# Plain float32 products for the first values, and reciprocal roots by logarithm and exponential on ScalarE

## The chip, the cores and the metric

The kernel runs on one core of a Trainium2 chip. The engines of the core are TensorE (PE in the profile; PEld is its weight load), VectorE (DVE), ScalarE (ACT), GpSimd (POOL) and SyncE (SP), which issues most of the transfers. The metric is the device time of one execution in microseconds; lower is better. The kernel before takes 343.04 us, the median of three runs (342.67 to 343.07).

## What is computed

A decoder trunk on 256 tokens of width 1024, all in float32: a mixer of four attention kinds with four heads each, a cross-attention into 256 memory tokens, and a squared-ReLU MLP of width 4096. Cut to what matters here:

```python
def rmsnorm(x, g):
    y = x * lax.rsqrt(jnp.mean(x * x, axis=-1, keepdims=True) + NORM_EPS)
    return y * g

x = x + hybrid_mixer(rmsnorm(x, g_mix), w_in, g_group, sinks, w_out, rel_table)
x = x + memory_cross_attention(rmsnorm(x, g_cross), rmsnorm(mem, g_mem), w_xq, w_xkv, w_xo)
x = x + jnp.square(jax.nn.relu(rmsnorm(x, g_mlp) @ w_up)) @ w_down
return rmsnorm(x, g_final)
```

In the mixer, h @ w_in gives queries, keys and values of the groups a (dilated windows), b (stick-breaking), c (sliding window with sinks) and d (one causal block). Each group's result is normed as well, y * rsqrt(mean(y * y) + NORM_EPS), before the output projection.

## The kernel before

The 256 tokens are two row tiles of 128, x0 and x1. The width of 1024 is eight blocks of 128, over which a product sums. A product in full precision is made of three float32r products: each operand is split into a high part (`hi`, a rounding copy on ScalarE, line 314 for weights, 400 for activations) and a residue (`lo`, a subtraction on VectorE, lines 315 and 401), and hi*hi, hi*lo and lo*hi are added in PSUM (lines 424 to 426). Weights come in halves of 512 KB into one of four `raw` buffers (line 300), and each half is split into two of the fifteen `w` buffers.

Start: x0, the first half of the weights of group a's values (`av`), x1, the second half, and the query weights `aq` are loaded in that order by SyncE, the first gain by ScalarE's queue. Forty small products on a tile of zeros (line 366, called warm-ups below) run on TensorE meanwhile, wherever nothing else can. Each row tile is transposed by TensorE (line 407), multiplied by the gain on VectorE (line 417) into `tmp`, and split. The norm's root does not stand before the products: it scales queries and keys as a row (`rq`, `rk`, lines 462 and 463; `spread` on line 459 turns it by a transpose) and values as a column (line 498). The values of group a are 48 products for both tiles (line 495), with a piece of the relative bias between them (line 471).

A reciprocal root (`rstd_of`, lines 383 to 388): ScalarE squares a row with a running sum (line 392), VectorE makes the variance (line 385), GpSimd raises it to the power -0.5 (line 386). There are sixteen of these: two at the start, two for the memory rows, eight for the attention results (four groups, two tiles), two before the cross-attention, two before the MLP, where GpSimd also squares the root (line 819). The final norm does the same on lines 1001 and 1003, and scales the rows on lines 1014 and 1017.

The order of each engine's instructions comes from a planner (`Plan`): every operation is recorded with an estimated cost and what it reads and writes, and a list scheduler puts them in order by these costs, by ranks and by when buffers come free. So an operation with another engine or cost moves others too. Each engine runs its list strictly in that order. From about 165 us on the MLP runs: sixteen units of 256 hidden columns, fourteen of them by a scheme of seven products in place of eight (`load_s`, `up_s`, `down_s`), the first and the last by the plain scheme.

## Time and profile before

| | |
|---|---|
| median of the runs | 343.04 us |
| the profiled execution | 342.83 us |
| its span | 340.9 us |
| TensorE busy with products | 329.0 us (97%) |
| VectorE busy | 299.2 us (88%) |
| ScalarE busy | 231.7 us (68%) |
| GpSimd busy | 27.6 us (8%) |
| transfers | 59.88 MB, mean 176 GB/s |

The span goes from the first instruction to the last; the rest of the execution's time lies around it. The busy time of an engine is the time in which it had an instruction running. Products are pipelined, so that the duration on record of one is longer than the distance to the next; in a dense stream the distance is what a product costs. A view by stretches tells what is full where, and the list of waits what an engine stood idle for.

### The profile page before, as it was taken

Reading aid. Unit: us, or ns where it says so; the run is one execution under the profiler, and the core shown is the slowest. Engines: PE = TensorE matmul, PEld = TensorE weight load, DVE = VectorE, ACT = ScalarE, POOL = GpSimd, SP = SyncE. Lnnn points to the kernel's source line nnn. Section 1 sums busy time; section 2 is a strip of 40 time slices with the busy share of each in tenths; the row PEclk is TensorE's granted clock in tenths of the full one; section 3 lists DMA queues with packets and bytes.
Section 4 is the critical chain, followed back from the end, with each engine's and each line's share of the span. In section 5 each row is a group of like instructions: output and inputs, shape, how many; then the busy total and the mean of one; then the engine's idle time right before and its main releaser. Section 6 shows DMA issues by size and latency. Waiting matters only on the chain.

```text
span 340.9 us, 6081 instructions
## 1 busy us (share of the span) xinstructions
PE 329.0 (97%) x2326; PEld 302.4 (89%) x2326; DVE 299.2 (88%) x488; ACT 231.7 (68%) x371; POOL 27.6 (8%) x46
## 2 busy tenths in 40 slices
PE   7799999999999999999999999999999999999992
PEld 6699899999898789998998899888999889998882
DVE  3758779779998499878999999999999999999994
ACT  4578857369794476883885876778668678665822
POOL 6422000000121002200020000000000000000000
PEclk9999999999999999999999999999999999999997
DMA  7989775640137334847743646476566574644003
GB/s 257 317 254 330 218 201 181 236 137 0 64 109 214 112 122 147 268 143 227 268 139 109 222 160 232 147 229 198 178 225 211 178 248 159 212 123 125 3 0 123
DMA packets 39757, 59.88 MB, mean 176 GB/s; under 512 B 1990, under 2 KB 32896, under 8 KB 39728
## 3 DMA queue, kind: packets, MB, share of 16 engines
q1 hardware_dynamic: 38928, 57.49, 52.2%
q0 software_dynamic: 640, 1.80, 1.8%
q8 instruction: 18, 0.29, 0.4%
q10 hardware_dynamic: 160, 0.20, 0.2%
q14 instruction: 11, 0.09, 0.1%
HBM read 58.42 MB, written 1.07 MB: 175 GB/s over the span
## 4 chain that ended last, share of the span: by engine, by line
PE 57%; DVE 21%; ACT 7%; issue 7%; DMA 5%; POOL 1%; SPq 0%; POOLq 0%; ACTq 0%; DVEq 0%
PE ps L425 9%; PE ps L424 9%; PE ps L426 9%; PE acc L424 8%; PE acc L425 8%; PE acc L426 8%; DVE w L315 5%; DVE w L872 4%; DMA raw<-in_w_in_dram 3%; PE ps L557 3%; PE ps L407 3%; DMA x<-in_x_dram 2%; ACT w L314 2%; DVE tmp L878 2%; POOL rstd L386 1%
## 5 line engine op out<-in xcount | busy, mean ns | idle before, releaser
L315 DVE TENSOR_TENSOR w<-raw,w 128x1024 fp32r<-128x1024 f32 x72 | 86.1, 1218 | 11.6 <-ACT w L314 8.2
L314 ACT ACTIVATE w<-raw 128x1024 fp32r<-128x1024 f32 x72 | 73.9, 1053 | 14.8 <-PE acc L425 7.6
L425 PE MATMUL ps<-hTlo,w 128*128 128x256 f32 x256 | 72.1, 281 | 0.0
L424 PE MATMUL ps<-hThi,w 128*128 128x256 f32 x256 | 71.9, 281 | 0.0
L426 PE MATMUL ps<-hThi,w 128*128 128x256 f32 x256 | 71.8, 281 | 0.0
L424 PEld LDWEIGHTS ps<-hThi,w 128*128 128x128 f32 x256 | 48.2, 188 | 0.7
L425 PEld LDWEIGHTS ps<-hTlo,w 128*128 128x128 f32 x256 | 48.1, 188 | 0.6
L426 PEld LDWEIGHTS ps<-hThi,w 128*128 128x128 f32 x256 | 48.3, 189 | 0.0
L424 PE MATMUL acc<-w,yThi 128*128 128x512 f32 (+1 forms) x112 | 45.2, 404 | 0.0
L425 PE MATMUL acc<-w,yThi 128*128 128x512 f32 (+1 forms) x112 | 43.7, 390 | 0.0
L426 PE MATMUL acc<-w,yTlo 128*128 128x512 f32 (+1 forms) x112 | 43.7, 390 | 0.0
L871 ACT ACTIVATE w<-tmp 128x1024 fp32r<-128x1024 f32 x28 | 29.6, 1058 | 15.6 <-DVE tmp L881 13.1
L424 PE MATMUL acc<-hThi,w 128*128 128x256 f32 x128 | 36.6, 286 | 0.0
L425 PE MATMUL acc<-hTlo,w 128*128 128x256 f32 x128 | 36.1, 282 | 0.0
L426 PE MATMUL acc<-hThi,w 128*128 128x256 f32 x128 | 35.8, 280 | 0.0
L872 DVE TENSOR_TENSOR w<-tmp,w 128x1024 fp32r<-128x1024 f32 x28 | 34.1, 1218 | 0.0
L386 POOL TENSOR_TENSOR rstd<-var,mhalf 128x1 f32<-128x1 f32 x16 | 15.9, 998 | 137.5 <-DVE var L385 89.4
L426 PEld LDWEIGHTS acc<-w,yTlo 128*128 128x128 f32 x112 | 21.0, 188 | 5.0
L425 PEld LDWEIGHTS acc<-w,yThi 128*128 128x128 f32 x112 | 21.1, 188 | 4.2
L424 PEld LDWEIGHTS acc<-w,yThi 128*128 128x128 f32 x112 | 21.1, 188 | 4.0
L424 PEld LDWEIGHTS acc<-hThi,w 128*128 128x128 f32 x128 | 24.1, 188 | 0.4
L426 PEld LDWEIGHTS acc<-hThi,w 128*128 128x128 f32 x128 | 24.2, 189 | 0.0
(189 smaller groups left out, 708.6 us busy)
## 6 DMA issues: line engine op xcount, KB each, us to landing
raw<-in_w_up_dram SPq DMA_DIRECT2D x32, 512.0 KB, 4.2
raw<-in_w_in_dram SPq DMA_DIRECT2D x22, 512.0 KB, 4.9
hThi<-in_w_down_dram SPq DMA_DIRECT2D x14, 512.0 KB, 3.4
hTlo<-in_w_down_dram SPq DMA_DIRECT2D x14, 512.0 KB, 4.1
raw<-in_w_out_dram SPq DMA_DIRECT2D x8, 512.0 KB, 3.4
raw<-in_w_xkv_dram SPq DMA_DIRECT2D x4, 512.0 KB, 3.5
raw<-in_w_down_dram SPq DMA_DIRECT2D x4, 512.0 KB, 4.3
w<-dstrip POOLq DMA_DIRECT2D x3, 512.0 KB, 8.3
```

The source lines that it names most:

```text
L314: act(1024, lambda raw=raw, hi=hi: nc.scalar.activation(hi.t, raw.t, AF.Copy), [raw], [hi])
L315: dve(1024, lambda raw=raw, hi=hi, lo=lo: nc.vector.tensor_sub(lo.t, raw.t, hi.t.bitcast(F32)), [raw, hi], [lo])
L386: pool(0.5, lambda: nc.gpsimd.tensor_tensor(r.t, v.t, mhalf.t, op=ALU.pow), [v, mhalf], [r])
L407: nc.tensor.transpose(dst[:, tsl(k)], view()[:, tsl(k)], ident.t)
L424: nc.tensor.matmul(dst, lh, rh, start=start, stop=False)
L425: nc.tensor.matmul(dst, lh, rl, start=False, stop=False)
L426: nc.tensor.matmul(dst, ll, rh, start=False, stop=stop)
L557: nc.tensor.matmul(view()[:, h, :], z[:, i, :], v[:, j, kv(h), :], start=j == 0, stop=j == len(pT[h]) - 1)
L871: act(512 * n, lambda: nc.scalar.activation(hi.t, view(), AF.Copy), [key], [hi])
L872: dve(512 * n, lambda: nc.vector.tensor_sub(lo.t, view(), hi.t.bitcast(F32)), [key, hi], [lo])
L878: dve(1024, lambda: nc.vector.tensor_sub(s.t, raw[:, 1:2].to_broadcast([P, 2, 512]), raw[:, 0:4:3]), [raw], [s])
```

## The change

The first values (group a) are no longer computed from split operands: their weights go as they come into two `w` buffers (`load_whole`), and the products take the gained, transposed rows `tmp` themselves, in plain float32, 16 of them with a planned cost of 0.43 us each. So the weights of `av` are not split; x0 and x1 still are, for queries and keys. The planner's cost of x1's load is raised. The load of the first gain is recorded ahead of x0's; it stays on ScalarE's queue.

A reciprocal root is made by two activations on ScalarE, exp(-0.5 * ln(ssq / n + eps)), with eps as a column in memory (it stands in the buffer named `mhalf`). The MLP's scale, the square of the root, becomes a variance and a reciprocal on VectorE. The factor for the cross-attention's queries (`rs`) moves from GpSimd to VectorE. In the final norm the logarithm takes the sum's last part and, as its bias, the part so far. The first addition to the relative bias no longer waits for the second tile's variance.

```diff
--- before.py
+++ after.py
@@ -32,6 +32,7 @@
 FRONT = 20.0
 EARLY = 1.0
 NUDGE = 0.5
+FULL = 0.43
 LAST = 2
 SPLIT = 640
 LASTC = 768
@@ -326,7 +327,7 @@
         xt.append(buf(f"x{t}", [P, D]))
 
     def load_x(t):
-        dma(P * D * 4, lambda: nc.sync.dma_start(xt[t].t, a["x"][0, tsl(t), :]), [], [xt[t]])
+        dma(P * D * (4 + 3 * t), lambda: nc.sync.dma_start(xt[t].t, a["x"][0, tsl(t), :]), [], [xt[t]])
 
     GN = ("g_mix", "g_cross", "g_mem", "g_mlp")
     grow = [buf("grow0", [KB, P]), buf("grow1", [3 * KB, P])]
@@ -336,14 +337,21 @@
         dma(4096, lambda: eng.dma_start(
             grow[i > 0].t[j:j + KB, :], a[GN[i]][0].rearrange("(k p) -> k p", p=P)), [], [(grow[i > 0], i)])
 
+    whole = []
+
+    def load_whole(part):
+
+        whole.append(buf("w", [P, KB // 2, 256], F32, SPL))
+        dma(P * D * 4, lambda: nc.sync.dma_start(whole[part].t, units["av"][:, 4 * part:4 * part + 4]), [], [whole[part]])
+
+    load_gain(0, nc.scalar)
     load_x(0)
-    load_gain(0, nc.scalar)
-    load("av", 0)
+    load_whole(0)
     load_x(1)
-    load("av", 1)
-    ident, mhalf, warm = buf("ident", [P, P]), buf("mhalf", [P, 1]), buf("warm", [P, 512], BF16)
+    load_whole(1)
+    ident, eps, warm = buf("ident", [P, P]), buf("mhalf", [P, 1]), buf("warm", [P, 512], BF16)
     pool(0.5, lambda: make_identity(nc, ident.t), [], [ident])
-    pool(0.05, lambda: nc.gpsimd.memset(mhalf.t, -0.5), [], [mhalf])
+    pool(0.05, lambda: nc.gpsimd.memset(eps.t, EPS), [], [eps])
     dve(512, lambda: nc.vector.memset(warm.t, 0.0), [], [warm])
     onehot, rel, smask = buf("q", [32, STRIP], F32, 2), buf("rel", [32, NROW]), buf("k", [NROW, STRIP], F32, 2)
     sink, nsink = buf("sink", [P, 4]), buf("nsink", [P, 4])
@@ -378,19 +386,20 @@
     gains_T(0)
 
 
-    last = []
-
     def rstd_of(ssq, n):
-        v, r = buf("var", [P, 1], F32, 4), buf("rstd", [P, 1], F32, 16)
-        dve(1, lambda: nc.vector.tensor_scalar(v.t, ssq.t, 1.0 / n, EPS, op0=ALU.mult, op1=ALU.add), [ssq], [v])
-        pool(0.5, lambda: nc.gpsimd.tensor_tensor(r.t, v.t, mhalf.t, op=ALU.pow), [v, mhalf], [r])
-        last.append(v)
+        r = buf("rstd", [P, 1], F32, 16)
+        v = buf("var", [P, 1], F32, 4)
+        act(1, lambda: nc.scalar.activation(v.t, ssq.t, AF.Ln, bias=eps.t, scale=1.0 / n), [ssq, eps], [v], 1)
+        act(1, lambda: nc.scalar.activation(r.t, v.t, AF.Exp, scale=-0.5), [v], [r], 1)
         return r
 
-    def rstd_row(src, view, n, behind=[]):
+    def ssq_row(src, view, n, behind=[]):
         sq, ssq = buf("sq", [P, D], BF16, 1), buf("ssq", [P, 1], F32, 4)
         act(n, lambda: nc.scalar.activation(sq[:, 0:n], view(), AF.Square, accum_out=ssq.t), [src] + behind, [sq, ssq], 1)
-        return rstd_of(ssq, n)
+        return ssq
+
+    def rstd_row(src, view, n):
+        return rstd_of(ssq_row(src, view, n), n)
 
     def pair(tag, n, bufs):
         return tuple(buf(tag + x, [P, n, S], F32R, bufs) for x in ("hi", "lo"))
@@ -418,6 +427,7 @@
                 tmp[:, ks, :], pt.t.rearrange("p (k t) -> p k t", k=4), gT[g > 0][:, max(g - 1, 0), ks, None].to_broadcast([P, 4, P]),
                 op=ALU.mult), [pt, gT[g > 0]], [(tmp, n)])
             split_to(hl, (t, n), (slice(None), ks, tsl(t)), (tmp, n), lambda ks=ks: tmp[:, ks, :], 512)
+        return tmp
 
     def mm3(dst, l, r, start, stop):
         (lh, ll), (rh, rl) = l, r
@@ -446,9 +456,9 @@
 
 
     h1 = pair("hT", KB, 2)
-    r1 = []
+    g1, r1 = [], []
     for t in range(2):
-        gained_T(xt[t], 0, h1, t)
+        g1.append(gained_T(xt[t], 0, h1, t))
         r1.append(rstd_row(xt[t], lambda t=t: xt[t].t, D))
 
     rq, rk = buf("rq", [P, S]), buf("rk", [P, S])
@@ -469,7 +479,7 @@
     pst0 = pst()
     dstrip = buf("dstrip", [NROW, STRIP], pool=dram)
     pe(0.65, lambda: nc.tensor.matmul(pst0[:NROW, :STRIP], rel.t, onehot.t, start=True, stop=True), [rel, onehot], [pst0])
-    dve(STRIP, lambda: nc.vector.tensor_add(smask.t, pst0[:NROW, :STRIP], smask.t), [pst0, smask, last[-1]], [smask])
+    dve(STRIP, lambda: nc.vector.tensor_add(smask.t, pst0[:NROW, :STRIP], smask.t), [pst0, smask], [smask])
     dma_late(20000, lambda: nc.gpsimd.dma_start(dstrip.t, smask.t), [smask], [dstrip])
 
 
@@ -488,13 +498,10 @@
                 if gi:
                     proj(pv, lambda pv=pv: pv[:, 0:256], n + "v", h1, t)
                 else:
-                    for half in range(2):
-                        for p in ((0, 0), (1, 0), (0, 1)):
-                            for kk in range(4 * half, 4 * half + 4):
-                                w, j = wt("av", kk)
-                                pe(0.109, lambda p=p, kk=kk, w=w, j=j, t=t, pv=pv: nc.tensor.matmul(
-                                    pv[:, 0:256], h1[p[0]][:, kk, tsl(t)], w[p[1]][:, j], start=kk == 0 and p == (0, 0),
-                                    stop=kk == KB - 1 and p == (0, 1)), [w[p[1]], (h1[p[0]], (t, half))], [pv])
+                    for kk in range(KB):
+                        pe(FULL, lambda kk=kk, t=t, pv=pv: nc.tensor.matmul(
+                            pv[:, 0:256], g1[t][:, kk, :], whole[kk // 4][:, kk % 4], start=kk == 0, stop=kk == KB - 1),
+                            [whole[kk // 4], (g1[t], kk // 4)], [pv])
                 act(256, lambda t=t, pv=pv: nc.scalar.activation(
                     v[:, t, :, 0:E], pv[:, 0:256].rearrange("p (h e) -> p h e", h=4), AF.Copy, scale=r1[t].t),
                     [pv, r1[t]], [(v, t)], 1)
@@ -776,7 +783,7 @@
         residual(pacc[t], t)
         gained_T(xt[t], 1, h2, t)
         r2, rs = rstd_row(xt[t], lambda t=t: xt[t].t, D), buf("rs", [P, 1], F32, 2)
-        pool(0.1, lambda r2=r2, rs=rs: nc.gpsimd.tensor_scalar(rs.t, r2.t, -0.125, None, op0=ALU.mult), [r2], [rs])
+        dve(1, lambda r2=r2, rs=rs: nc.vector.tensor_scalar(rs.t, r2.t, -0.125, None, op0=ALU.mult), [r2], [rs])
         pq = pst()
         proj(pq, lambda pq=pq: pq[:, 0:256], "xq", h2, t)
         q2 = buf("yn", [P, 256], F32, 2)
@@ -814,9 +821,10 @@
         plan.nudge = 0.0
     plan.fixed = MLP_RANK + 1
     for t in range(2):
-        r = rstd_row(xt[t], lambda t=t: xt[t].t, D, list(h3))
         r3.append(buf("r3", [P, 1], F32, 2))
-        pool(0.1, lambda t=t, r=r: nc.gpsimd.tensor_tensor(r3[t].t, r.t, r.t, op=ALU.mult), [r], [r3[t]])
+        ssq, v = ssq_row(xt[t], lambda t=t: xt[t].t, D, list(h3)), buf("var3", [P, 1], F32, 2)
+        dve(1, lambda v=v, ssq=ssq: nc.vector.tensor_scalar(v.t, ssq.t, 1.0 / D, EPS, op0=ALU.mult, op1=ALU.add), [ssq], [v])
+        dve(1, lambda t=t, v=v: nc.vector.reciprocal(r3[t].t, v.t), [v], [r3[t]])
 
     plan.fixed = MLP_RANK
 
@@ -998,9 +1006,9 @@
                     dve(1, lambda ssq=ssq, pre=pre, c=c: nc.vector.scalar_tensor_tensor(
                         pre.t, ssq[:, c:c + 1], 1.0 / D, pre.t, op0=ALU.mult, op1=ALU.add), [(ssq, c), pre], [pre])
             else:
-                dve(1, lambda ssq=ssq, pre=pre, c=c, var=var: nc.vector.scalar_tensor_tensor(
-                    var.t, ssq[:, c:c + 1], 1.0 / D, pre.t, op0=ALU.mult, op1=ALU.add), [(ssq, c), pre], [var])
-                pool(0.5, lambda var=var, r=r: nc.gpsimd.tensor_tensor(r.t, var.t, mhalf.t, op=ALU.pow), [var, mhalf], [r])
+                act(1, lambda ssq=ssq, pre=pre, c=c, var=var: nc.scalar.activation(
+                    var.t, ssq[:, c:c + 1], AF.Ln, bias=pre.t, scale=1.0 / D), [(ssq, c), pre], [var], 1)
+                act(1, lambda var=var, r=r: nc.scalar.activation(r.t, var.t, AF.Exp, scale=-0.5), [var], [r], 1)
             plan.nudge = -1.0
             dve(c1 - c0, lambda cs=cs, x=x, ov=ov: nc.vector.tensor_mul(ov(), x[:, cs], g_final[:, cs]),
                 [(x, c0), g_final], [(o, n)])
```

What that does to the order, at three places. In the rows, a name such as w_147 is a buffer; the number behind it tells buffers apart.

TensorE at the start, around the transposes of the second row tile (x_0_132). Before, behind the last warm-up the transposes and then products of split parts:

```order
L366 LDWEIGHTS warm_70
L366 MATMUL acc_75<-warm_70 128x128
L407 MATMUL ps_177<-ident_65,x_0_132 128x128 x4
L407 MATMUL ps_185<-ident_65,x_0_132 128x128 x4
L495 MATMUL acc_194<-w_147,hThi_163 128x256 x4
L471 MATMUL ps_201<-q_73,rel_85 13x384
L495 MATMUL acc_209<-w_147,hThi_163 128x256 x4
```

Now, the place where the first plain products stand (tmp_134 is the gained x0, w_104 the first half of the value weights), between warm-ups:

```order
L374 LDWEIGHTS warm_70
L374 MATMUL acc_75<-warm_70 128x128
L502 MATMUL acc_151<-w_104,tmp_134 128x256 x4
L374 LDWEIGHTS warm_70
L374 MATMUL acc_75<-warm_70 128x128
L374 LDWEIGHTS warm_70
L374 MATMUL acc_75<-warm_70 128x128
```

Four plain products have moved ahead of the transposes of the second tile, which follow seven warm-ups later.

TensorE at the spread of the roots (rstd) and the first query product, line 424 before and 434 now. Before:

```order
L495 MATMUL acc_209<-w_147,hTlo_204 128x256 x2
L495 MATMUL acc_209<-w_173,hThi_163 128x256 x3
L459 MATMUL ps_261<-ident_65,rstd_175 128x128
L459 MATMUL ps_261<-ident_65,rstd_248 128x128
L495 MATMUL acc_209<-w_173,hThi_163 128x256
L495 MATMUL acc_209<-w_215,hThi_163 128x256 x4
L495 MATMUL acc_209<-w_215,hTlo_204 128x256
L495 MATMUL acc_194<-w_252,hThi_163 128x256 x4
L495 MATMUL acc_209<-w_215,hTlo_204 128x256 x3
L495 MATMUL acc_209<-w_252,hThi_163 128x256 x3
L424 MATMUL acc_291<-hThi_163,w_228 128x256
```

Now:

```order
L502 MATMUL acc_151<-w_166,tmp_134 128x256
L481 MATMUL ps_203<-q_73,rel_87 13x384
L469 MATMUL ps_209<-ident_65,rstd_143 128x128
L469 MATMUL ps_209<-ident_65,rstd_197 128x128
L502 MATMUL acc_151<-w_166,tmp_134 128x256 x3
L502 MATMUL acc_231<-w_104,tmp_188 128x256 x4
L434 MATMUL acc_245<-hThi_149,w_217 128x256
L435 MATMUL acc_245<-hTlo_155,w_217 128x256
```

Seven plain products stand between the second root's spread and the first query product, in place of sixteen products of split parts; the last four plain ones come later, between query products.

ScalarE at the end of the program, from the squares of the final norm (sq) to the output's transfer. Before:

```order
L991 ACTIVATE sq_4024,ssq_0_4025<-x_0_79 128x512 x2
L1017 ACTIVATE tmp_4019<-tmp_4019,rstd_4046 128x1024
L991 ACTIVATE sq_4065,ssq_1_4066<-x_0_132 128x512
L991 ACTIVATE sq_4065,ssq_1_4066<-x_0_132 128x256
L1017 ACTIVATE tmp_4060<-tmp_4060,rstd_4093 128x384
L1019 DMA out_dram<-tmp_4060 128x384
```

Now:

```order
L999 ACTIVATE sq_3980,ssq_0_3981<-x_0_82 128x512 x2
L1009 ACTIVATE var_3997<-ssq_0_3981,ssq_3990 128x1
L1011 ACTIVATE rstd_3999<-var_3997 128x1
L1025 ACTIVATE tmp_3975<-tmp_3975,rstd_3999 128x1024
L999 ACTIVATE sq_4022,ssq_1_4023<-x_0_132 128x512
L999 ACTIVATE sq_4022,ssq_1_4023<-x_0_132 128x256
L1009 ACTIVATE var_4047<-ssq_1_4023,ssq_4033 128x1
L1011 ACTIVATE rstd_4049<-var_4047 128x1
L1025 ACTIVATE tmp_4017<-tmp_4017,rstd_4049 128x384
L1027 DMA out_dram<-tmp_4017 128x384
```

The logarithm (line 1009) and the exponential (line 1011) stand behind each tile's last square, ahead of its scaling (line 1025, formerly 1017). Elsewhere on ScalarE a pair stands behind its square in the same way, at some places with other instructions between. On SyncE's queue the two loads of the memory rows have moved behind eight further weight loads and that of g_group.

## Rows read from the trace of the kernel before

**Rows 1.** The page's busy time, share of the span and instructions of each engine.

```profile
PE 329.0 (97%) x2326; PEld 302.4 (89%) x2326; DVE 299.2 (88%) x488; ACT 231.7 (68%) x371; POOL 27.6 (8%) x46
```

**Rows 2.** Stretches: us; busy PE, PEld, DVE, ACT, POOL; granted clock; transfers.

```profile
70.00:100.00 30.00, 29.48 (x246) 27.76 (x244) 28.30 (x77) 25.43 (x60) 2.56 (x3) 1.00 0.22 71
...
80.00:90.00 10.00, 9.91 (x84) 9.50 (x84) 9.72 (x32) 7.44 (x20) 0.90 (x2) 1.00 0.07 16
...
90.00:100.00 10.00, 9.57 (x76) 8.76 (x75) 9.85 (x27) 9.79 (x23) 1.66 (x2) 1.00 0.27 92
...
165.00:330.00 165.00, 165.00 (x1087) 150.32 (x1086) 163.04 (x220) 117.18 (x156) 2.91 (x4) 1.00 0.50 166
```

**Rows 3.** Timeline of TensorE: start, duration, line, operation, shape, count; idle before.

```profile
16.59 0.32 PE L459 MATMUL ps<-ident,rstd 128*128 128x128 f32 x1 [1.83 <-POOL rstd L386]
...
18.64 0.28 PE L424 MATMUL acc<-hThi,w 128*128 128x256 f32 x1
...
21.47 0.28 PE L424 MATMUL acc<-hThi,w 128*128 128x256 f32 x1
```

**Rows 4.** Timeline of GpSimd and VectorE in the same stretch.

```profile
13.48 3.05 POOL L386 TENSOR_TENSOR rstd<-var,mhalf 128x1 f32<-128x1 f32 x1 [4.52 <-DVE var L385]
...
13.78 2.34 DVE L315 TENSOR_TENSOR w<-raw,w 128x1024 fp32r<-128x1024 f32 x2
```

**Rows 5.** Timeline of TensorE: plain float32 products.

```profile
10.45 0.49 PE L471 MATMUL ps<-q,rel 32*13 32x384 f32 x1
...
10.45 0.81 PE L471 MATMUL ps<-q,rel 32*13 32x384 f32 x2
...
36.80 1.10 PE L557 MATMUL ps<-v,pT 128*128 128x65 f32 x8 [0.77 <-ACT pT L244]
...
37.72 0.37 PE L424 MATMUL acc<-hThi,w 128*128 128x256 f32 x1
```

**Rows 6.** Timeline of TensorE: transposes at the start and later.

```profile
4.27 1.09 PE L407 MATMUL ps<-ident,x 128*128 128x128 f32 x4 [0.36 <-DMA x<-in_x_dram]
...
8.49 0.90 PE L407 MATMUL ps<-ident,x 128*128 128x128 f32 x3 [0.17 <-DMA x<-in_x_dram]
...
8.75 1.29 PE L407 MATMUL ps<-ident,x 128*128 128x128 f32 x7
...
114.51 1.03 PE L407 MATMUL ps<-ident,tmp 128*128 128x128 f32 x8
```

**Rows 7.** Transfers: SyncE's issues, and sizes with us to landing by stretch.

```profile
2.18 1.68 SPq L300 DMA_DIRECT2D raw<-in_w_in_dram  x3
...
raw<-in_w_in_dram SPq DMA_DIRECT2D x1, 512.0 KB, 7.6
...
raw<-in_w_in_dram SPq DMA_DIRECT2D x1, 512.0 KB, 10.0
```

**Rows 8.** Groups of ScalarE by line and shape: count, busy, mean ns, idle before.

```profile
L314 ACT ACTIVATE w<-raw 128x1024 fp32r<-128x1024 f32 x72 | 73.9, 1053 | 14.8 <-PE acc L425 7.6 <-PE acc L426 4.0 <-DVE yn L692 2.4
...
L682 ACT ACTIVATE extra<-extra 128x4 f32<-128x4 f32 x2 | 0.4, 193 | 0.0
...
L498 ACT ACTIVATE v<-acc,rstd 128x256 f32<-128x256 f32 x6 | 2.8, 467 | 1.4 <-PE acc L495 1.3
...
L763 ACT ACTIVATE vx<-ps 128x256 f32<-128x256 f32 x2 | 0.7, 381 | 0.0
```

**Rows 9.** Timeline at the end of the span, VectorE, GpSimd and ScalarE.

```profile
335.25 0.08 DVE L987 DVE_READ_ACCUMULATOR2_ANT ssq<- 128x1 f32 x1
...
335.37 0.16 DVE L1001 SCALAR_TENSOR_TENSOR var<-ssq,ssq 128x1 f32<-128x1 f32 x1
...
335.44 0.42 DVE L1005 TENSOR_TENSOR tmp<-x,w 128x256 f32<-128x256 f32 x1
...
335.61 0.66 POOL L1003 TENSOR_TENSOR rstd<-var,mhalf 128x1 f32<-128x1 f32 x1 [3.70 <-DVE var L1001]
...
336.30 0.62 ACT L1017 ACTIVATE tmp<-tmp,rstd 128x384 f32<-128x384 f32 x1 [2.20 <-POOL rstd L1003]
```

## The prediction

> **What bounds the kernel now.** I read the busy shares first [rows 1]: TensorE is busy for 97% of the span, VectorE for 88%, ScalarE for 68%. Shares are means over stages, so the stretches come next [rows 2]. From 165 to 330 us TensorE is busy 165.00 of 165 us and VectorE 163.04: nothing can be won there, since the change takes no product out of it. From 70 to 100 us all three are nearly full (29.48, 28.30 and 25.43 of 30 us); at 90 to 100 us ScalarE has 0.2 us of 10 left. So the time is the moment when TensorE's stream becomes dense, plus its work, plus a tail. The start is read from TensorE's timeline [rows 3]: it stands still until 16.59 us, idle 1.83 us for the reciprocal root of the second row tile, and begins the queries at 18.64. The cause is one line on [rows 4]: the power on GpSimd ran from 13.48 for 3.05 us, beside VectorE's two residue subtractions (13.78, 2.34 us). The tail shows the same operation on the end of everything [rows 9].
>
> The profiled execution took 342.83 us, 340.9 of them span; the median of the runs is 343.04. I make the sum against the profile and add the 0.21 us at the end.
>
> **The value products.** Before: 48 products (two row tiles, eight k blocks, three split pairs). Their spacing is that of the first query products: 24 of them from 18.64 to 21.47 us [rows 3], 0.118 us each, so 48 x 0.118 = 5.7 us. After: 16 plain ones. The only plain float32 product with a long moving side is the one of the relative bias, 13 x 384 [rows 5]: two records for one product, the first 0.49 us long and both together 0.81, so a record adds 0.32 us for 384 columns, 0.213 for 256, and a product 0.427. That has only 13 weight columns; whether loading 128 of them hides is told by the products of probabilities and values: eight records of 65 columns from 36.80 to 37.72, 0.115 us each [rows 5]. If load and product were serial, a 256-column record would cost the product's 0.213 plus at most that 0.115, 0.33 us. I take 0.427 us a product, since the long product is nearer in columns, and keep 0.66 as the upper end. Sum: 16 x 0.427 = 6.8 us. TensorE's work grows by 1.1 us; the gain must come from the start.
>
> **The start, step by step.** The SP queue keeps its order up to the queries' weights: x0, first value half, x1, second value half, queries. Only the memory rows drop behind eight more weight loads and g_group, and need no place until their transposes (after 114 us) [rows 6]. Landing, as before: x0 at 4.3 us, x1 at 8.5 [rows 6], second value half at 2.18 + 7.6 = 9.8, the last query half by about 3.5 + 10.0 = 13.5 [rows 7]. At first the array runs at half rate: four transposes took 1.09 us at 4.27 and eight 1.03 at 114.51; the seven from 8.75 took 1.29, so the rate rose near 9.4 us [rows 6]. By these durations the clock stood at the lower of its two levels, 1.2 GHz, before and at 2.4 after.
> TensorE's new order puts four plain products of x0 ahead of x1's transposes. With eight transposes of x0 at 0.21 from 4.4 (the gains are turned first) and four warm-ups, they begin at 6.65. Each costs 2 x 0.427 us while the rate is half: 3.2 of them until 9.4, the rest at full rate, 9.75. Seven warm-ups (0.4), x1's transposes (0.9) and four warm-ups (0.2) end at 11.25, where x1 before was done at 9.80. From there all is full rate: one plain product (11.7), bias product (12.35), spreading both roots (12.6), three products (13.85), four products of x1 (15.56), then query products; four plain products (1.7) stand among those. Equivalent start of the queries: 15.56 + 1.7 = 17.27, against 18.64 + 0.12 (one value product was left over). **Front: -1.5 us.**
> Whether something else is late there: x1's root leaves ScalarE at about 10.2 (square from 8.5, about 1.05 us as the copies of 1024 columns [rows 8], the read of its sum 0.2, then logarithm and exponential), ahead of its use at 12.4. Query weights: ScalarE copies them at 13.2 to 14.25 behind the spread root, VectorE subtracts until 15.5 (1.22 us, half of the 2.34 in [rows 4]). That is ready 0.1 us before 15.56, the second half (17.4) just as the one plain product behind the first ends. No slack, so the gain can shrink by some tenths, not vanish. VectorE loses two residues (2.4 us) and ScalarE two copies of 1053 ns [rows 8].
>
> **The reciprocal roots.** Of the eighteen roots sixteen turn from a variance on VectorE (0.16 us [rows 9]) and a power on GpSimd into two activations. The nearest row is the 128 x 4 exponential, 193 ns [rows 8]; a pointer operand adds 467 - 381 = 86 ns (v with a scale, vx without). So logarithm 0.28, exponential 0.19, pair 0.47 us. The MLP's two become a variance and a reciprocal on VectorE (by the same row about 0.16 us each), and are wanted only by the additions behind the last mixed unit, some 150 us later: hidden. Twelve pairs fall between 20 and 140 us: 5.6 us more on ScalarE, 1.9 less on VectorE. Where ScalarE idles they cost nothing; where it is full (90 to 100 us in [rows 2]) what queues behind them is late: the copies of weights, the exponentials of probabilities. Against this, the path from square to scaled row loses a hop to VectorE and GpSimd. I take zero, with 1.3 us to either side: three of the twelve pairs without cover (1.4), or, the other way, TensorE's idle 0.52 us at 70 to 100 us and a wait for ScalarE's copy such as the 0.77 before 36.80 [rows 5] mended by the new order.
> GpSimd's queue: the bias strip's DMA no longer stands behind the 3.05 us power, and the masks arrive some 3 us earlier; nobody waits.
> **Tail.** Reduction ends at 335.33, scaling starts at 336.30 [rows 9]: 0.97 us for variance, power and hops. After: a hop of 0.05 (0.03 to 0.08 in these rows), then 0.47: start at 335.86. **Tail: -0.4 us.** The last product with g_final (0.42 us, VectorE's only work behind the reduction) moves up into the variance's place, ends at 335.8 and stays covered.
>
> **Sum:** 342.83 - 1.5 - 0.4 = 340.9, plus 0.21: **341.1 us**.
>
> **Rivals.** (a) *The rate rises late.* If x1's transposes still run at half rate, the front plain products end at 10.06, warm-ups at 10.8, transposes at 12.5; the rest (6.2 us) gives 18.7: the whole front gain is gone, 342.6. Against it: the plain products are denser work than before's.
> (b) *It rises early.* If the products run at full rate from 6.65, they end at 8.4, x1's transposes at 9.6, and queries stand at 15.9 less what their weights hold up (0.2): front -2.7, time 339.9. In this trace x1's transposes alone saw the rise, behind 16 warm-ups. The Trainium skill, TensorE: Matmul & The Clock Gate, Part 4, says that transpose mode does not count as busy in the way a matmul does; by that rule the new stretch, with real products in place of warm-ups and before the transposes, would favour (b), 339.9. The trace here neither shows nor refutes it, so I give it a chance and not the forecast.
> (c) *Slower: ScalarE's queue.* If the pairs stand on the path in the attention stage, each costs 0.47 us there. Four exposed pairs (1.9 us) eat the gain, six make the kernel slower; all eight of the attention give 341.1 + 3.8 = 344.9. For it: 9.79 of 10 us busy at 90 to 100 us. Against: 7.44 in the ten before, 68% over the span, and roots that took 0.66 us on GpSimd with nothing beside them [rows 9] and 3.05 beside VectorE [rows 4].
> (d) *Slower: plain products serial with their weight loads.* 16 x (0.66 - 0.427) = 3.7 us more: 344.8.
> (e) *Not what it says*, another table load between logarithm and exponential: the instruction order has a single load, at the start. Left out.
>
> **Chances.** Forecast 0.50, (a) 0.15, (b) 0.17, (c) 0.13, (d) 0.05. A measurement of this kernel can tell 0.2%, 0.69 us, from no change. Faster: the forecast and (b), 0.67. Same: (a) and a little of (c), 0.17. Slower: the rest of (c), and (d), 0.16. The forecast alone spans 339.8 to 342.4 with the middle's 1.3 us; the range goes down to (b) with a part of that, 339.5, and up past (a) to 343.6, which leaves most of (c), (d) and a sliver below, about 0.2.
>
> **What would show it.** Right: no gap of TensorE at the spread of the roots, queries' first product near 15.6 with plain records 0.21 us apart, density from 11 us on, final scaling 0.5 us behind the reduction. (a) or (b): the duration of x1's transposes and of the first plain records. (c): TensorE waiting for ScalarE's copies or probabilities between 70 and 110 us, with its idle sum there above the 0.5 us of [rows 2]. (d): records 0.33 us apart. Wrong altogether if the queries begin early and the dense stretch from 165 us still starts when it did: then the middle gave the gain back.

## The result and the profile after

The changed kernel is slower: 347.46 us, the median of four runs (346.68 to 350.57), against 343.06 for the kernel before on the same chip. The ratio is 1.013, with a 95% interval of 1.009 to 1.018. The forecast was 341.1 us, faster. The profiled execution took 346.68 us, 344.9 of them span, against 340.9 before, so 4.0 us are to be found.

The profile is that of the fastest of the four. Its busy times differ by a few us from [rows 1], except that GpSimd lost its powers:

```profile
PE 332.4 (96%) x2310; PEld 304.7 (88%) x2310; DVE 296.0 (86%) x473; ACT 237.0 (69%) x402; POOL 7.7 (2%) x24
```

TensorE's timeline at the start of the changed kernel (columns as in [rows 3]). The first plain products come at 6.40, the roots are spread at 11.40 without the gap of 1.83 us, and the queries begin at 14.51, not at 18.64 (one plain product is two records):

```profile
6.40 2.35 PE L502 MATMUL acc<-w,tmp 128*128 128x256 f32 x8
8.58 0.55 PE L374 MATMUL acc<-warm 128*128 128x128 bf16 x7
8.97 1.05 PE L416 MATMUL ps<-ident,x 128*128 128x128 f32 x8
9.85 0.39 PE L374 MATMUL acc<-warm 128*128 128x128 bf16 x4
10.08 0.65 PE L502 MATMUL acc<-w,tmp 128*128 128x256 f32 x2
...
11.40 0.43 PE L469 MATMUL ps<-ident,rstd 128*128 128x128 f32 x2
11.67 3.19 PE L502 MATMUL acc<-w,tmp 128*128 128x256 f32 x14
14.51 0.47 PE L434 MATMUL acc<-hThi,w 128*128 128x256 f32 x1
```

So the front gain is there, and larger than forecast. The rows of the stretches behind it (us; busy PE, PEld, DVE, ACT, POOL; granted clock; share of the transfer engines; GB/s), after first, then before:

```profile
25.00:28.00 3.00, 3.00 (x22) 2.56 (x21) 2.52 (x3) 0.01 (x1) 0.00 (x0) 1.00 1.04 345
28.00:31.00 3.00, 1.77 (x14) 1.24 (x13) 0.95 (x1) 2.02 (x4) 0.00 (x0) 1.00 1.10 348
31.00:35.00 4.00, 3.67 (x19) 3.67 (x20) 3.29 (x13) 3.90 (x10) 0.00 (x0) 0.57 0.88 257
```

```profile
25.00:28.00 3.00, 3.00 (x28) 3.00 (x27) 1.53 (x3) 2.69 (x6) 2.36 (x4) 1.00 0.91 310
28.00:31.00 3.00, 3.00 (x27) 3.00 (x27) 2.94 (x6) 1.59 (x4) 0.00 (x0) 1.00 1.01 295
31.00:35.00 4.00, 4.00 (x37) 3.74 (x37) 3.87 (x12) 3.37 (x7) 0.00 (x0) 1.00 1.05 344
```

From 28 to 31 us TensorE works 1.77 of 3.00 us, and from 31 to 35 its granted clock is 0.57 on the mean: for part of that stretch it stood at 1.2 GHz. The list of waits names ScalarE's and VectorE's halves of a weight split, and ScalarE's timeline says for what these waited:

```profile
PE acc L434 <- ACT w L315: 0.8, 1, 0.8
PE acc L436 <- DVE w L316: 0.8, 1, 0.8
```

```profile
23.95 1.06 ACT L315 ACTIVATE w<-raw 128x1024 fp32r<-128x1024 f32 x1 [3.66 <-DMA raw<-in_w_in_dram]
28.96 1.06 ACT L315 ACTIVATE w<-raw 128x1024 fp32r<-128x1024 f32 x1 [3.95 <-DMA raw<-in_w_in_dram]
```

The weights come late, with the transfer engines full (a share of 1.04 to 1.10 from 25 to 31 us). What else is in flight is told by GpSimd's queue, after and then before: the masks (512 KB each, 128 for `past`) go out 6 us earlier. The bias strip that they are read from is stored 3.45 us earlier, and the wait for its landing takes 3.61 us in place of 6.07.

```profile
13.05 0.52 POOL L483 DMA_DIRECT2D dstrip<-k  x1 [7.71 <-DVE nsink L478]
17.17 0.80 POOL L724 DMA_DIRECT2D w<-dstrip  x1 [3.61 <-DMA dstrip<-k]
17.96 0.54 POOL L724 DMA_DIRECT2D past<-dstrip  x1
18.49 1.50 POOL L724 DMA_DIRECT2D w<-dstrip  x2
```

```profile
16.50 0.56 POOL L473 DMA_DIRECT2D dstrip<-k  x1
23.13 0.80 POOL L717 DMA_DIRECT2D w<-dstrip  x1 [6.07 <-DMA dstrip<-k]
...
24.46 1.50 POOL L717 DMA_DIRECT2D w<-dstrip  x2
```

To see where the rest went, I read the start of the same product in each kernel: A, the first score product of group a; B, the first of its second tile; C, the first of the cross-attention; D and E, the first and the fourteenth unit's product of `pT` and `yThi` in the MLP. All are TensorE's timeline, in us, from the one profiled execution of each kernel.

| kernel | A | B | C | D | E | span | D to E |
|---|---|---|---|---|---|---|---|
| before | 31.27 | 34.85 | 143.18 | 180.98 | 318.08 | 340.9 | 137.10 |
| after | 28.00 | 35.54 | 145.11 | 183.81 | 322.21 | 344.9 | 138.40 |
| after, less before | -3.27 | +0.69 | +1.93 | +2.83 | +4.13 | +4.0 | +1.30 |
| values alone | 28.34 | 35.35 | 145.71 | 184.39 | 321.36 | 344.4 | 136.97 |
| roots alone | 32.35 | 37.42 | 144.14 | 183.46 | 320.74 | 343.2 | 137.28 |
| after, masks held | 27.92 | 32.36 | 141.96 | 180.66 | 319.06 | 341.8 | 138.40 |
| after, middle roots on GpSimd | 27.56 | 34.79 | 143.75 | 182.49 | 318.99 | 341.5 | 136.50 |
| roots alone, masks held | 29.84 | 33.50 | 140.57 | 179.35 | 316.64 | 339.1 | 137.29 |

Four losses stand in the third line: 4.0 us between A and B, 1.2 to C, 0.9 to D, and 1.3 in the MLP, where no product had been touched. The MLP's loss is a steady 0.1 us a unit.

The stretches from B to C and from C to D, before and then after, tell what the second and the third loss are:

```profile
34.85:143.18 108.33, 107.04 (x813) 99.85 (x812) 89.99 (x186) 74.03 (x144) 9.90 (x13) 1.00 0.49 150
143.18:180.98 37.80, 37.30 (x294) 35.26 (x292) 34.04 (x55) 27.70 (x49) 2.91 (x4) 1.00 0.62 203
```

```profile
35.54:145.11 109.57, 108.11 (x824) 100.69 (x822) 89.97 (x179) 79.81 (x173) 0.12 (x1) 1.00 0.46 147
145.11:183.81 38.70, 37.17 (x289) 35.22 (x290) 33.79 (x55) 27.47 (x48) 0.00 (x0) 1.00 0.57 191
```

From B to C TensorE's idle time is nearly the same (1.29 and 1.46 us); it is busy 1.07 us longer, with 11 products more. By their names six are split products (0.12 us each) and three warm-ups, which TensorE's new order runs behind B and no longer ahead of it, and two are transposes from behind C. So about 0.9 us of this loss is work moved past B, and B comes 0.9 us earlier than it would with the same work ahead of it. From C to D the idle time grows from 0.50 to 1.53 us: that loss is a wait.

The tail gained what was forecast; VectorE's last reading of the sum and ScalarE's pair and scaling, after:

```profile
339.38 0.08 DVE L995 DVE_READ_ACCUMULATOR2_ANT ssq<- 128x1 f32 x1
...
339.49 0.29 ACT L1009 ACTIVATE var<-ssq,ssq 128x1 f32<-128x1 f32 x1 [1.35 <-DVE ssq L995]
339.82 0.20 ACT L1011 ACTIVATE rstd<-var 128x1 f32<-128x1 f32 x1
340.05 0.61 ACT L1025 ACTIVATE tmp<-tmp,rstd 128x384 f32<-128x384 f32 x1
```

From the end of the reading (339.46) to the scaling it is 0.59 us, in place of the 0.97 of [rows 9]. From E to the end only 0.1 us came off.

### The profile page after: what moved, and what is told of

It reads as the page before. It is cut to its first block, busy times and chain, and to the rows that moved or that the text cites. A ratio compares the mean times of both kernels' runs of the same rounds, so it can differ in the third digit from the quotient of the medians.

```text
span 344.9 us, 6038 instructions
## 1 busy us (share of the span) xinstructions
PE 332.4 (96%) x2310; PEld 304.7 (88%) x2310; DVE 296.0 (86%) x473; ACT 237.0 (69%) x402; POOL 7.7 (2%) x24
## 3 DMA queue, kind: packets, MB, share of 16 engines
HBM read 58.42 MB, written 1.07 MB: 172 GB/s over the span
## 4 chain that ended last, share of the span: by engine, by line
PE 77%; ACT 7%; DMA 6%; DVE 5%; SPq 1%; issue 1%; ACTq 0%; DVEq 0%
PE ps L436 13%; PE ps L435 13%; PE ps L434 13%; PE acc L434 11%; PE acc L436 11%; PE acc L435 11%; DMA raw<-in_w_in_dram 6%; PE ps L564 3%; PE ps L416 2%; ACT qs L604 2%; DVE w L316 1%; ACT w L315 1%; PE ps L546 1%; ACT ks L592 1%; ACT w L684 1%
## 5 line engine op out<-in xcount | busy, mean ns | idle before, releaser
L316 DVE TENSOR_TENSOR w<-raw,w 128x1024 fp32r<-128x1024 f32 x70 | 83.6, 1219 | 14.5 <-ACT w L315 14.2
L315 ACT ACTIVATE w<-raw 128x1024 fp32r<-128x1024 f32 x70 | 71.7, 1050 | 17.1 <-DMA raw<-in_w_in_dram 9.8
L434 PE MATMUL acc<-hThi,w 128*128 128x256 f32 x128 | 38.0, 297 | 0.8 <-ACT w L315 0.8
L436 PE MATMUL acc<-hThi,w 128*128 128x256 f32 x128 | 36.9, 289 | 0.8 <-DVE w L316 0.8
L434 PEld LDWEIGHTS acc<-hThi,w 128*128 128x128 f32 x128 | 24.9, 194 | 1.4 <-ACT w L315 1.0
L436 PEld LDWEIGHTS acc<-hThi,w 128*128 128x128 f32 x128 | 24.8, 194 | 1.0 <-DVE w L316 1.0
L435 PEld LDWEIGHTS acc<-hTlo,w 128*128 128x128 f32 x128 | 24.9, 194 | 0.1
```

Of the source, the lines that this page charges most:

```text
L315: act(1024, lambda raw=raw, hi=hi: nc.scalar.activation(hi.t, raw.t, AF.Copy), [raw], [hi])
L316: dve(1024, lambda raw=raw, hi=hi, lo=lo: nc.vector.tensor_sub(lo.t, raw.t, hi.t.bitcast(F32)), [raw, hi], [lo])
L434: nc.tensor.matmul(dst, lh, rh, start=start, stop=False)
L435: nc.tensor.matmul(dst, lh, rl, start=False, stop=False)
L436: nc.tensor.matmul(dst, ll, rh, start=False, stop=stop)
```

## The experiments

Each was run beside the kernel before on the same chip. Ratios are to that kernel, with 95% intervals; before's own medians lay between 342.65 and 343.05 us, its single runs between 341.25 and 346.47. The ratios are not the quotients of the medians, which lie up to 0.3% away (1.0073 in place of 1.0042 for the middle roots on GpSimd). The theory to test: the earlier masks take memory bandwidth from group b's weights just when TensorE, ahead of its old schedule, needs them.

### The parts, and the masks alone

**The kernel before, again.** No edit.

> The kernel before, run once more beside the others of this group, to have its trace from the same chip. Two readings of the creep between 165 and 330 us are open: 256-column products of the dense stretch stood 0.1200 us apart in the trace of the changed kernel and 0.1178 in that of the kernel before. If that belongs to the chip that ran it, this trace shows the spacing that the changed kernels of this group show, within 0.0005 us; if it belongs to the kernel, this one shows 0.1178 and they show 0.1200. Total 342.7 to 345.

Measured: 345.04 us in its one run, 512- and 256-column products 0.2332 and 0.1178 us apart, as in the first trace of this kernel; the changed kernel has 0.2332 and 0.1199. (Such spacings are, here and below, the mean distance of the starts of neighbouring products of that width from 190 to 310 us.) So the longer 256-column spacing belongs to the kernel, not to the chip. This run was slow for another reason: TensorE waited 2.49 us at 37.59 for a copy that stood behind a late weight transfer (2.48 us). The kernel before too stands on the edge there.

**The values alone**: of the diff the parts on `FULL`, `load_x`, `load_whole`, `g1` and the plain products; all roots as before. **The roots alone**: the rest of the diff; the 48 products as before.

> Only the plain products of the first values; all roots stay on GpSimd. Theory 1 (collision: TensorE reaches group b's weights earlier, while the masks' transfers, sent about 6 us earlier than before, and the g_group load take memory bandwidth from those weights, and TensorE then falls to 1.2 GHz for some 3 us): the masks still start before 19 us, TensorE still waits near 28 to 32 us and its clock still falls, so the kernel is 1 to 3 us slower than before, about 345.5. Theory 2 (ScalarE's order in the cross-attention, where a copy of weights and an activation of queries stand between the exponentials; this kernel has that order too): the wait of 1 us near 150 us is there as well, and is part of that sum. Rival (the logarithm and exponential pairs on ScalarE make the loss): without them this kernel keeps the front gain and is 0.5 to 2 us faster than before, about 341.5.

> Only the roots on ScalarE; the first values stay 48 split products. Theory 1: the front gains about 1.5 us, since the GpSimd power of 3.05 us is gone and the roots are spread without a wait, but TensorE comes no more than that earlier to group b's weights, and their loads stand behind the two of the memory rows as before, so there may be a wait near 30 us, at most the front gain; the tail gains 0.4; total 341.5 to 343. Theory 2: no wait of 1 us near 150 us, since the four exponentials stand together as before. Rival (the pairs on ScalarE make the loss): slower than before by 2 to 4 us, with TensorE waiting for ScalarE between 40 and 150 us.

Measured: the values alone 345.75 us (1.0076, 1.0054 to 1.0099), the roots alone 343.69 (1.002, 0.999 to 1.005). In both, masks went out early (17.42 and 17.96 us), and in both TensorE starves and then slows down. The values alone, then the roots alone:

```profile
28.00:31.00 3.00, 2.38 (x17) 1.62 (x16) 0.46 (x2) 1.45 (x3) 0.00 (x0) 1.00 1.09 345
31.00:35.00 4.00, 3.24 (x17) 3.00 (x16) 3.31 (x12) 3.89 (x10) 0.00 (x0) 0.65 0.83 239
```

```profile
28.00:31.00 3.00, 2.26 (x17) 1.85 (x16) 0.53 (x1) 1.06 (x1) 0.00 (x0) 1.00 1.09 345
31.00:35.00 4.00, 3.04 (x18) 2.70 (x19) 3.53 (x7) 3.26 (x4) 0.00 (x0) 0.74 0.75 237
```

Either part gains at the front (the queries begin at 15.45 and 16.31 us) and gives it back. The parts cost 0.8% and 0.2%, both together 1.3%; the intervals leave open whether that is more than the sum. The rival that the pairs on ScalarE make the loss falls: without any pair the values alone lose 0.8%, and all the pairs without the values 0.2%, no clear change.

**The masks held.**

```diff
         def go():
             src = dstrip.t
+            if gi == 2:
+                for _ in range(24):
+                    nc.gpsimd.memset(hold.t, 0.0)
 ...
```

> The changed kernel with one edit: 24 fills of a spare 128 x 512 buffer on GpSimd, about 0.5 us each, stand ahead of the mask of group c, so that its transfer and that of group d start some 12 us later, near 30 us, behind group b's weights. The order on the other engines is as in the changed kernel. Theory 1 (collision): the weights of group b arrive earlier, the waits of 0.8 us near 30 and 31 us and the fall of the clock go, the total falls by 2 to 3.5 us against the changed kernel, to about 344.5. Rival (memory is full by other transfers, or ScalarE's order makes the wait): the waits stay, total within 0.7 us of the changed kernel. If the masks come too late for groups c and d, TensorE waits for them near 45 or 60 us instead.

Measured: 344.67 us (1.0052, 1.0026 to 1.0078), 2.8 us below the changed kernel. The masks of c and d start at 31.80, ScalarE has the late weights at 26.08 and not at 28.96, and the hole, TensorE's idle time near 30 us, is gone:

```profile
17.86 13.99 POOL L728 MEMSET hold<- 128x512 f32 x24
31.80 1.50 POOL L729 DMA_DIRECT2D w<-dstrip  x2
```

```profile
26.08 1.06 ACT L315 ACTIVATE w<-raw 128x1024 fp32r<-128x1024 f32 x1 [1.38 <-DMA raw<-in_w_in_dram]
```

```profile
28.00:31.00 3.00, 3.00 (x28) 2.88 (x29) 2.67 (x11) 2.90 (x7) 2.71 (x6) 1.00 0.69 195
31.00:35.00 4.00, 4.00 (x33) 3.65 (x33) 3.84 (x14) 3.18 (x8) 2.25 (x4) 1.00 1.01 385
```

At B this kernel is 3.18 us ahead of the changed one, whose list on TensorE it shares: that is the collision's price. It is 2.49 us ahead of before, of which 0.9 is the work moved past B; the front gain that is kept is 1.6. The Trainium skill, DMA: Bandwidth & Descriptors, section Issuing engines are not separate DMA queues, says that transfers of all issuing engines run on the same 16 engines and interleave. These two traces agree: with 1 MB held back on GpSimd's queue, a weight load of SyncE's queue was ready 2.9 us sooner.

**The same on the roots alone.** The same edit.

> The kernel with the roots alone on ScalarE, and with the 24 fills on GpSimd ahead of the mask of group c. Theory 1: that kernel reached the queries 2.3 us earlier than before and lost 3.4 us between 18 and 35 us, since its masks too went out from about 16 us and not from 23; with two of them held the waits near 30 us and the fall of the clock go, and the total falls by 2 to 3 us, to about 341, below the kernel before. Rival (its loss there comes from the memory rows, which stand in front of the weights in its queue): still a wait near 30 us, total as without the fills, 343.7.

Measured: 341.24 us (0.9947, 0.992 to 0.9974): 0.5% faster than the kernel before, 2.45 us below the roots alone.

**The same on the kernel before**, as a control: first with 12 fills.

> The kernel before with 12 fills of a spare buffer on GpSimd (about 6 us) ahead of the mask of group c, which so starts near 31 us and not at 24.5. It tells whether holding the masks is a gain of its own. Theory 1: before, TensorE reaches group b's weights 2 to 4 us later and the masks start at 23.1, so that the collision is small: total within 0.7 us of before. Rival (the masks take as much from the kernel before): 1 us or more faster than before, and the gain of 1.8 us of the kernel with roots on ScalarE and held masks would then be mostly the holding.

Measured: 349.36 us (1.019), and it tells nothing on the masks. VectorE shows why: it stood for 8 us, since the roots of the memory rows are GpSimd's work in this kernel and were now queued behind the fills.

```profile
33.08 1.57 DVE L746 TENSOR_SCALAR tmp<-tmp,rstd 128x1024 f32<-128x1024 f32 x2 [7.99 <-POOL rstd L386]
```

Second, with eight fills and both masks moved behind those two roots, in the planner's `issue`:

```diff
+        held = [op for op in order if op["mark"] and op["eng"] == "POOL"]
...
+        at = [i for i, op in enumerate(order) if i >= at and op["eng"] == "POOL"][1]
+        order[at + 1:at + 1] = held
```

> The kernel before with the masks of groups c and d sent behind the two roots of the memory rows on GpSimd and behind eight fills, so that they start near 31 us and not at 24.5, and no root waits for the fills. Theory 1: within 0.7 us of before (the collision is small there). Rival: 1 us or more faster; then the gain of 1.8 us of the kernel with roots on ScalarE and held masks is mostly the holding.

Measured: 342.11 us (0.9982, 0.9966 to 0.9998). The masks start at 30.11. Holding is worth 0.2% there, just clear of none; of the 0.5% of the roots with masks held, the larger part is then the roots' by these two ratios, though their intervals (0.02 to 0.34% and 0.26 to 0.8%) overlap.

### The middle

TensorE's two longest waits from 10 to 165 us in the changed kernel are in the middle, the first near 150 us and the second near 94; before has neither:

```profile
PE ps L546 <- ACT w L808: 1.1, 1, 1.1
PE ps L611 <- ACT pT L245: 1.0, 1, 1.0
```

**The twelve middle roots back on GpSimd.**

```diff
     def rstd_of(ssq, n):
+        if len(r1) == 2:
+            v, r = buf("var", [P, 1], F32, 4), buf("rstd", [P, 1], F32, 16)
+            dve(1, lambda: nc.vector.tensor_scalar(v.t, ssq.t, 1.0 / n, EPS, op0=ALU.mult, op1=ALU.add), [ssq], [v])
+            pool(0.5, lambda: nc.gpsimd.tensor_tensor(r.t, v.t, mhalf.t, op=ALU.pow), [v, mhalf], [r])
+            return r
```

> The changed kernel with the twelve roots in between (attention, memory rows, cross-attention) back on GpSimd; the first two and the final norm's stay on ScalarE. The masks go out as early as in the changed kernel, so the loss near 30 us stays. Theory 4 (prediction's rival c, in small: pairs on a full ScalarE cost 0.9 us between 88 and 123 us): the wait of 1.0 us near 94 us goes, total falls by 0.5 to 1 us, to about 346.7. Here high part and residue of the MLP stand 8192 bytes apart as well but at multiples of 64 bytes: by theory 3 the spacing stays at 0.120, and if the place within 64 bytes decides, it is 0.118 and the total falls by 1.3 us more. Rival: the pairs cost nothing, no difference.

Measured: 345.47 us (1.0042, 1.0011 to 1.0074). The wait for `pT` near 94 us is gone, and B to C takes 108.96 us in place of 109.57, with the same products: the pairs cost 0.6 us there (0.7 with the masks held: 108.86 in the last kernel below, 109.60 with the pairs). The MLP took 136.50 us, 1.9 less than in the changed kernel. The profiled run, 343.26 us, is one of the two fastest of ten. TensorE starves in it too, but its granted clock does not fall:

```profile
28.00:31.00 3.00, 1.38 (x12) 0.85 (x8) 1.22 (x1) 2.36 (x5) 0.00 (x0) 1.00 1.09 348
31.00:35.00 4.00, 3.73 (x25) 3.07 (x26) 3.35 (x13) 3.93 (x9) 0.00 (x0) 1.00 0.92 296
```

**The cross-attention.** The wait near 150 us is for the second pair of exponentials of the first tile: on ScalarE a weight copy (147.71 us, 1.06) and three query copies (148.76, 1.16) stand between the two pairs, where before all four ran in a row. The values alone, without any pair, have the wait as well (1.2 us). Three edits at this place, each on the changed kernel. The four exponentials of the first tile (marked) in a row again, what stood among them on ScalarE behind them:

```diff
+            late = not op["mark"] and (op["eng"] == "ACT" or op["pre"] & moved)
+            (back if late else stay).append(op)
...
+        order[at[0]:at[-1] + 1] = stay + back
```

> The changed kernel with one place of ScalarE's list reordered: the four exponentials of the first tile in the cross-attention stand in a row again, as in the kernel before, ahead of the copy of weights and the four query copies that stood among them. Nothing else moves on any engine. Theory 2: the wait of 1.1 us at 149.9 us (transposes of probabilities for the second exponentials) goes; the copies behind it come 0.6 us later each, and nobody on the path waits for them; total falls by 0.8 to 1.2 us, to about 346.4. Rival (a weight product further on was the real limit and now waits for the copy): the wait moves to another row between 150 and 156 us, total unchanged.

Measured: 349.66 us (1.019); the wait grew and moved:

```profile
PE ps L555 <- ACT vx L779: 2.1, 1, 2.1
```

The weight copy between them moved behind `vx` (whose copies are marked too):

```diff
+            late = op["eng"] == "ACT" and op["cost"] > 0.9 or op["pre"] & moved
```

> The changed kernel with one copy of weights on ScalarE (1.05 us, and its residue on VectorE) moved in the cross-attention from between the two pairs of exponentials of the first tile to behind the two copies of vx, as in the kernel before. Putting the four exponentials ahead of that copy with the query copies left behind it had only moved the wait to vx (2.1 us). Theory 2, mended (the weight copy that stands one place earlier is what the exponentials, query copies and vx are late for): the wait of 1.1 us near 150 goes, from #16 of the products ks by qs to the first transposes of the MLP stage the kernel takes 0.8 us less, total 0.8 us below the changed kernel. Rival: the wait moves again, to the weights of that copy or to pT behind it; total unchanged.

Measured: 348.37 us (1.018). C to D took 40.2 us, not 38.7. ScalarE now waits for TensorE, which gives it the second tile's queries late:

```profile
148.01 1.15 ACT L613 ACTIVATE qs<-ps 64x256 fp32r<-64x256 f32 x3 [0.95 <-PE ps L620]
```

So TensorE's own list was tried, by the rank of one pair of transposes:

```diff
         pt = pst()
+        plan.nudge += -0.5 * t
         transpose(pt, q2, lambda q2=q2: q2.t, 2, [q2])
+        plan.nudge -= -0.5 * t
```

> The changed kernel with one planner number: the transposes of the second tile's queries in the cross-attention have their rank lowered by 0.5. In the changed kernel they stand ahead of the first tile's scores and hold one of the four ps buffers, so that the second score group stands behind seven groups of value products; here both score groups stand in a row and the transposes behind, as in the kernel before. Theory 6 (TensorE's own list makes ScalarE late there): from the first score product of the cross-attention (#16 of ks by qs) to the first transposes of the residual stream behind it (#37 of ident by x) the kernel takes 17.7 us, as before, in place of 18.5; no wait of 1 us near 150; total about 0.8 us below the changed kernel. Rival (the stage is limited by ScalarE's work): 18.4 us or more.

Measured: 347.88 us (1.0138); its profile had a wider hole near 30 us (a wait of 3.5 us). C to D took 38.46 us, where the changed kernel takes 38.70 and before 37.80. By these traces a quarter of the 0.9 us is TensorE's list. The rest is in the wait for ScalarE, but none of the edits to ScalarE's list won it back, so that its cause is argued and not shown.

### The MLP: where buffers lie

**The residues 128 bytes further.** A spare tile of 32 words is allotted ahead of the first `hTlo`; the edits below have other tags and sizes:

```diff
+            if self.tag == "hTlo" and self.seq == 0:
+                self.pool.tile([P, 32], F32, tag="gap", name="gap", bufs=1)
```

> The changed kernel with 128 bytes of unused memory ahead of the residues of the activations (hTlo), so that in the MLP the high part and the residue stand 8320 bytes apart in each partition, as in the kernel with the values alone, and not 8192 as in the changed kernel; no instruction differs. In the two kernels with a distance of 8192 (the changed kernel and the one with held masks) 256-column products of the MLP stand 0.120 us apart, in the four others (11968, 8320 and 11328 bytes) 0.1178. Theory 3 (the distance of 8192 between the operands that TensorE reads in turn costs the 2 ns): the spacing falls to 0.118, the first unit of seven products to the last one (#0 to #13 of the products that begin with pT and yThi) takes 137.1 us in place of 138.4, and the total falls by 1.3 us, to about 346.1. Rival (something in the code of the changed kernel, such as its order, makes the spacing): still 0.120, total unchanged.

Measured: 347.58 us (1.0132), D to E 138.32 us, 256-column products 0.1193 us apart and not 0.1178. The distance of 8192 bytes is not the cause.

**Everything from `hThi` on 32 bytes further.**

> The changed kernel with 32 bytes of unused memory ahead of the activations' high parts (hThi): they, the residues, the raw weights, pT and the yT pairs all lie 32 bytes further in each partition, where the kernel with the middle roots on GpSimd has them; no instruction differs. The distance between high part and residue, 8192 bytes, has been ruled out as the cause of the spacing (8320 bytes gave the same). Theory 5 (the place of the buffers within 64 bytes sets the spacing of the products): as in that kernel the MLP runs faster; one unit takes 10.50 us in place of 10.64 (the products that begin with pT and yThi, #0 to #13, 136.5 us in place of 138.4), total 1.9 us below the changed kernel. Rival (the order of VectorE's and ScalarE's work beside the products sets it): unit unchanged at 10.64 us, total unchanged.

Measured: D to E 136.50 us, from the two rows below: 1.9 us less with not one instruction changed. The total, 346.63 us (1.0113, 1.006 to 1.0165), hides part of it, since its runs spread from 344.83 to 348.51, and its profile has a wait of 3.9 us near 30 us.

```profile
187.08 0.39 PE L436 MATMUL ps<-pT,yThi 128*128 128x512 f32 x1
...
323.58 0.39 PE L436 MATMUL ps<-pT,yThi 128*128 128x512 f32 x1
```

**`pT` and the yT pairs 32 bytes further**, in the kernel before, and in the roots alone with masks held:

> The kernel before with 32 bytes of unused memory ahead of pT, so that pT and the yT pairs lie at 32 and not at 0 within 64 bytes; the h pairs stay. No instruction differs. Theory 5 (place within 64 bytes): 512-column products of the MLP go from 0.2329 to 0.2285 us, 256-column ones stay at 0.1178; one unit takes 10.45 us in place of 10.54, 14 units and the ends 1.3 to 1.5 us less; total about 341.5. Rival: no change in spacing and time.

> The kernel with the roots alone on ScalarE and the masks held (341.2), with the same 32 bytes ahead of pT. By theory 5 512-column products go from 0.2336 to 0.229 and the total falls by 1.3 to 1.5 us, to about 339.8, the fastest of all here and about 1% below the kernel before. Rival: 341.2.

Measured: the first has 512-column products 0.2285 us apart and D to E 135.92, as expected (342.17 us, 0.9986, 0.9962 to 1.0009: the total shows no clear gain); the second 0.2331, D to E 137.19 and no gain (341.38 us, 0.9945). So the place within 64 bytes is not it either. Over all traces one quantity fits, the distance of the yT pairs from the `w` buffers modulo 256 bytes, by the addresses that the programs were built with:

| distance yT - w, mod 256 | kernels | 512-column spacing, us |
|---|---|---|
| 224 | before, values alone, after | 0.2328 to 0.2332 |
| 128 | roots held, 32 bytes | 0.2331 |
| 96 | roots alone, roots held, after with 128 bytes | 0.2338 to 0.2339 |
| 0 | after and before shifted, middle roots on GpSimd | 0.2285 to 0.2287 |

`pT` moves with the yT pairs in all of these. But the gain is in the products of yT and `w`: two such in a row stand 0.2279 to 0.2281 us apart in the last line and 0.2329 to 0.2344 in the others, while those beside a product of `pT` follow no such order (0.2292 to 0.2344).

**Set to 0 on the fastest kernel**, by 160 bytes; and the residues of h as well:

> The kernel with the roots alone on ScalarE and the masks held (341.2 to 341.4), with 160 bytes of unused memory ahead of pT, so that the yT pairs lie at the same place within 256 bytes as the w buffers (distance 0; with no bytes it is 96 and with 32 bytes 128). No instruction differs. Theory 5, mended (the distance between yT and w modulo 256 bytes sets the spacing of the 512-column products): 0.2285 us in place of 0.2332 to 0.2336, the MLP 1.4 to 1.5 us shorter, total 339.8. Rival (something else that the kernels with 0.2285 share): 0.233, 341.3.

> As the kernel with 160 bytes, and with the residues of h (hTlo) at distance 0 from w modulo 256 bytes too (it is 64 there); the high parts of h are at 0 already. By theory 5, mended, the 512-column products stand 0.2285 us apart here as well; for the 256-column ones the traces so far give 0.1177 where only the high parts are at 0 and 0.1200 where neither is, so that 0.1165 is possible: another 0.7 us, total 339.1. Rival (the residues, a third of those products, do not matter): 0.1177, total as with 160 bytes.

Measured: with 160 bytes 0.2290 us and 340.13 us (0.9911, 0.9878 to 0.9943), the fastest kernel of all, D to E 135.98:

```profile
179.42 0.40 PE L427 MATMUL ps<-pT,yThi 128*128 128x512 f32 x1
...
315.40 0.40 PE L427 MATMUL ps<-pT,yThi 128*128 128x512 f32 x1
```

With the residues moved too, the 512-column products keep 0.2291, but the 256-column ones go from 0.1178 to 0.1198 and the total to 341.52. The distance predicts the first kind; for the second it does not.

**The values, mended**: middle roots on GpSimd, masks held, the weight copy moved.

> The plain products of the first values with all that the runs point to: roots of attention, memory rows and cross-attention on GpSimd, those of the start and of the final norm on ScalarE, masks of groups c and d held by 24 fills, and the weight copy of the cross-attention in its old place. Sum from the runs so far: 345.5 (middle roots on GpSimd) less 2.8 (masks held) less 0.8 (copy) = 341.9, and less up to 1.5 where the front gain of 2.4 us is kept whole: 340.4 to 341.9, below the kernel before. Rival (the front gain goes elsewhere, such as to a wait for group c's mask): 343 or more.

Measured: 343.45 us (1.0006, 0.9983 to 1.003), no more than even. At B it is 2.2 us ahead of before; by C 1.7, and by D, behind the weight copy that did not help, 0.7 us late.

## Why the prediction was wrong

**Right:** TensorE, not a share of busy time, sets the end; no gap at the spread; plain records 0.20 us apart (14 of them from 11.67 to 14.51), against the 0.213 assumed, with the weight load hidden; the pair at 0.49 us (0.29 and 0.20), against 0.47; the tail at -0.38 us from reading to scaling, against -0.4. Rivals (d) and (e) did not happen.

**Mis-sized:** the front. The clock rose early: eight records of x0 took 2.18 us from 6.40, and x1's eight transposes 0.88, where seven had taken 1.29 before. With four plain products still to come at 14.51 (the 24 records listed above are twelve products of the sixteen), the equivalent start is 14.51 + 4 x 0.41 = 16.15, 2.6 us ahead of 18.64 + 0.12, not 1.5. That is rival (b), at -2.7. The rule that the prediction cites there from the Trainium skill, TensorE: Matmul & The Clock Gate, Part 4, that transpose mode does not count as busy in the way a matmul does, agrees with this; no run here tests it by itself. Of the 2.6 us the kernel with held masks keeps 1.6 of like work at B; where the other 1.0 went is not traced.

**The step that failed:** "the masks arrive some 3 us earlier; nobody waits". They went out 6 us earlier, since the strip was stored 3.45 us sooner, as forecast, and also landed sooner; that was taken for a gift, and what the masks collide with was not asked. The working followed SyncE's queue up to the queries' weights and stopped. Behind them stand group b's weights, wanted 3 us sooner than before, in the stretch where the transfer engines were at 0.91 to 1.05 already. Held masks give back 3.2 us at B.

**Also wrong:** the middle at zero with 1.3 us to either side. It lost 2.1 from B to D. Of that 0.9 is work moved past B, no loss; the other 1.2 is idle time of TensorE, 0.2 of it to C and 1.0 from C to D, where the wait for ScalarE's exponentials near 150 us is and some 0.2 is TensorE's list. The pairs do cost 0.6 to C (rival (c) in small, at the place it named), nearly outweighed there by waits of before that are gone, such as the 0.77 us before 36.80. And "nothing can be won there" for the MLP: the range had no room for 1.3 us from moved buffers. The 1.3 lie in the 256-column products, 624 of them between D and E, each 0.0020 us further apart than before (0.1199 and 0.1178). Shown is that 32 bytes of shift, without any change of instructions, take 1.9 us off the changed kernel's MLP. Which of its own buffers' moves brought the 1.3 is not shown.

In the sum over before: -1.6 us of the front left at B for like work, +3.2 collision, +1.2 from B to D, +1.3 in the MLP, -0.1 behind it, together the +4.0 of the two spans.

The range ended at 343.6: rivals (c) and (d) were the only slow mechanisms and were mostly left above it. A rival built on the transfers at 20 to 35 us was missing.
